# Background work of a hybrid encoder layer in half-width tiles of their own, first statistics by products with ones, folds in another order

## The chip, the cores and the metric

One core of one Trainium2 chip (trn2) runs the kernel. The metric is the device time of one execution in microseconds; all operands are float32 in memory. The kernel before took 2555.42 us (median of three runs, 2549.77 to 2566.65).

## The reference

One encoder layer over 2560 tokens of 1024 channels: a prompt of 512 and a sample of 2048, with the same weights. Heads: 16 for queries, 4 for keys and values, of 64 channels; window of 128 tokens to each side.

```python
h = rmsnorm(x, norm_pre)
z = h @ w_in                       # 1024 -> 6656: pool_u, pool_g, q, k, v, attn_g, merge
pooled = multiscale_pool(pool_u)   # means over 2, 4, 8, 16 tokens, minus u
pb = (pooled @ w_pool_group, by group of 256) * pool_scale * silu(pool_g)
ab = windowed_attention(rope(q), rope(k), v, sink) * silu(attn_g)
m = sigmoid(merge_1) * (pb @ w_pool_proj) + sigmoid(merge_2) * (ab @ w_attn_proj)
y = x + rmsnorm(m @ w_out, norm_post)
```

## The kernel before

**Numbers.** A float32 operand is split into a high part (ScalarE casts, L105) and a low part (VectorE subtracts, L106), `hi_lo`. A product is three matmuls, high x high, high x low, low x high (`mm3`, L141 to L143).

**Phase 1** is the input projection, over three blocks of tokens (`BLOCKS`: 768, 896, 896). A block runs 26 pairs of output units of 128 channels. A pair is seven products (M1 to M7 in `ORDER`, a step each, 12 matmuls of half a block's width) on sums and differences of the weights' and the input's quarters, a scheme of Strassen's kind. The weights of a pair come into an R tile (and half_tile A21, or, from the second block on, ready sums in a Q tile), and each step's weight is split into a w tile. A pair's result goes from PSUM into two z tiles (`Post.start`; L391 adds) and is finished there: rotation of keys and queries (`Rope`), values transposed and stored (`Values.tr_steps`), SiLU, gates, pooling (`Pool`). The first two pairs of a block (keys, values) run step by step in turn, as do the last two. The pooling maps are folded into the weights before and during the first two pairs (`fold`: eight items of three split tiles and 24 matmuls each; results go out over h tiles).

**Background work** hangs beside a pair's steps (`hook(s, i, j, f)`: block, pair, step). `beside` loads at step j and forms at step j + 3. It is: the next block's statistics (sums of squares of x by rows, L222, then `rstd`, and `prep_r`, which spreads the roots over partitions by transposes, L239); the next block's normalised input in seven combinations, stored to memory (`later_load`, `later_form`) and fetched at the change of block through h tiles (`fetch_operand`); the first block's pooling, put off to the second and third (`Pool.again`, `later`); and the splits of the three phase-2 weights (`split_load`, `split_form`). All of it uses z tiles.

**Phase 2** runs the pool projection, attention, attention projection and output projection over blocks of 512 tokens. The change doesn't touch its code.

**Tiles.** z: six of 4 KB per partition; h: four of 2 KB; u: four of 2 KB; R: three of 6 KB; Q: two of 8 KB; w: seven (`NW, NZ, NH, NR = 7, 6, 4, 3`). A tile is free again when its last reader is done, a store's landing included.

**What sets the order.** TensorE's order is the program's, written out by hand; `run` loads weights up to seven w tiles ahead of the step that uses them. The other engines and both DMA queues are ordered before the run by the framework's scheduler, with its own estimates of when tiles come free; so their order is near the program's and not the same (in the trace VectorE forms sums of the pair weights between pieces of the first block's input). At run time each engine takes its list in order. All loads are issued by SP's queue, all stores (`store`, L99) by POOL's.

**Start.** `first` loads the identity and norm_pre, loads the first block's x by rows into six z tiles (L216), squares them on ScalarE, loads the first fold's weights, then the transposed input (four z tiles; two in a spare R, two more z) and two pairs' weights.

## Time and profile before

| | |
|---|---|
| median of three runs | 2555.42 us |
| profiled execution | 2564.07 us, its span 2562.3 us |
| TensorE busy in the span | 2361.5 us |
| VectorE, ScalarE, POOL busy | 1778.3, 1156.8, 446.3 us |
| mean granted clock of TensorE | 0.963 of full |
| moved by DMA | 611.51 MB, mean 239 GB/s |

PE is TensorE, PEld its weight loads, DVE VectorE, ACT ScalarE, POOL GpSimd, SP SyncE, whose queue issues the loads. Busy times include no waiting. A wait is put down to the semaphore that came last.

### The profile page before, as it was taken

How to read it: one execution, taken by the hardware profiler on the slowest of the kernel's cores; microseconds unless marked ns; L12 is line 12 of the kernel's file. 1: busy time of each engine (PE TensorE's matmuls, PEld its weight loads, DVE VectorE, ACT ScalarE, POOL GpSimd, SP SyncE). 2: the span in 40 equal slices, each digit the busy share in tenths (PEclk: the TensorE clock that was granted, in tenths of full speed). 3: DMA queues.
4: the chain of work that ended last, by engine and by line, in shares of the span. 5: the costliest groups of instructions: out<-in, count | busy, mean ns of one | idle time of the engine just before them, and what ended most of it. 6: DMA issues, size and time to landing. Idle time of an engine off the chain costs nothing.

```text
span 2562.3 us, 34370 instructions
## 1 busy us (share of the span) xinstructions
PE 2361.5 (92%) x11668; PEld 2099.0 (82%) x11668; DVE 1778.3 (69%) x3346; ACT 1156.8 (45%) x2461; POOL 446.3 (17%) x961
## 2 busy tenths in 40 slices
PE   4889999989999989578999899899999999989998
PEld 3889999978888888577889887778788878878887
DVE  6667788765677677557677757788488578668732
ACT  5444343634433335233444336566366366546511
POOL 2322222030112110323222201110110111011011
PEclk7989999999999999889999999999999999999999
DMA  7566877664565547667666668777777887867784
GB/s 280 185 243 205 301 256 256 231 211 177 183 244 182 214 176 254 214 231 259 237 239 242 228 223 280 239 260 272 251 254 245 278 271 252 288 227 256 239 299 168
DMA packets 189953, 611.51 MB, mean 239 GB/s; under 512 B 27089, under 2 KB 34513, under 8 KB 179793
## 3 DMA queue, kind: packets, MB, share of 16 engines
q1 hardware_dynamic: 146464, 428.55, 50.6%
q0 software_dynamic: 43312, 180.76, 18.2%
q8 instruction: 92, 1.51, 0.2%
q14 instruction: 85, 0.69, 0.1%
HBM read 428.49 MB, written 180.72 MB: 238 GB/s over the span
## 4 chain that ended last, share of the span: by engine, by line
PE 42%; DMA 8%; DVE 8%; issue 3%; ACT 2%; POOL 1%; SPq 0%; POOLq 0%; DVEq 0%; ACTq 0%
PE ps_g L141 6%; PE ps_g L143 6%; PE ps_g L142 6%; PE ps_s L141 4%; PE ps_s L142 4%; PE ps_s L143 4%; PE ps_t L1019 3%; PE ps_o L1034 2%; PE ps_o L1033 2%; PE ps_s L991 1%; PE ps_s L992 1%; DVE ps_s L995 1%; DVE Q L106 1%; DMA h<-ab 1%; DMA ab<-z 1%
## 5 line engine op out<-in xcount | busy, mean ns | idle before, releaser
L141 PE MATMUL ps_s<-arena,w 128*128 128x448 f32 (+1 forms) x1512 | 556.5, 368 | 112.5 <-DVE z L391 74.1
L142 PE MATMUL ps_s<-arena,w 128*128 128x448 f32 (+1 forms) x1512 | 550.6, 364 | 0.0
L143 PE MATMUL ps_s<-arena,w 128*128 128x448 f32 (+1 forms) x1512 | 549.8, 364 | 0.0
L141 PE MATMUL ps_g<-arena,w 128*128 128x512 f32 (+2 forms) x1264 | 493.8, 391 | 3.4 <-DVE u L860 2.2
L143 PE MATMUL ps_g<-arena,w 128*128 128x512 f32 (+2 forms) x1264 | 478.8, 379 | 0.0
L142 PE MATMUL ps_g<-arena,w 128*128 128x512 f32 (+2 forms) x1264 | 478.5, 379 | 0.0
L141 PEld LDWEIGHTS ps_s<-arena,w 128*128 128x128 f32 x1512 | 291.6, 193 | 143.0 <-DVE z L391 81.0
L105 ACT CAST w<-Q 128x512 fp32r<-128x512 f32 x312 | 192.8, 620 | 367.0 <-PE ps_s L143 323.6
L143 PEld LDWEIGHTS ps_s<-arena,w 128*128 128x128 f32 x1512 | 292.2, 193 | 17.5
L142 PEld LDWEIGHTS ps_s<-arena,w 128*128 128x128 f32 x1512 | 291.9, 193 | 16.8
L143 PEld LDWEIGHTS ps_g<-arena,w 128*128 128x128 f32 x1264 | 240.2, 190 | 35.6
L141 PEld LDWEIGHTS ps_g<-arena,w 128*128 128x128 f32 x1264 | 241.8, 191 | 23.2 <-DVE u L860 2.4
L142 PEld LDWEIGHTS ps_g<-arena,w 128*128 128x128 f32 x1264 | 241.6, 191 | 19.7
L997 ACT ACTIVATE R<-ps_s,nm 128x384 f32<-128x384 f32 (+1 forms) x320 | 179.5, 562 | 147.3 <-DVE nm L995 139.8
L106 DVE TENSOR_TENSOR w<-Q,w 128x512 fp32r<-128x512 f32 x312 | 213.5, 687 | 31.9 <-ACT w L105 20.4
L105 ACT CAST w<-R 128x512 fp32r<-128x512 f32 x234 | 144.8, 620 | 164.3 <-PE ps_s L143 139.9
L106 DVE TENSOR_TENSOR w<-R,w 128x512 fp32r<-128x512 f32 x234 | 160.3, 687 | 80.0 <-ACT w L105 76.8
L995 DVE CUSTOM_DVE_ANT_0 ps_s<-ps_s,mask,nsink 128x384 f32<-128x384 f32 (+1 forms) x320 | 189.0, 593 | 22.4 <-PE ps_s L992 19.7
L106 DVE TENSOR_TENSOR Q<-ps_t,Q 128x512 fp32r<-128x512 f32 x224 | 153.5, 686 | 14.1 <-ACT Q L105 11.7
L1019 PE MATMUL ps_t<-ident,R 128*128 128x128 f32 x896 | 139.9, 278 | 22.9 <-DVE Q L106 19.5
L391 DVE TENSOR_TENSOR z<-ps_s,u 128x448 f32<-128x448 f32 (+1 forms) x144 | 86.2, 598 | 100.8 <-PE ps_s L143 95.3
L1019 PEld LDWEIGHTS ps_t<-ident,R 128*128 128x128 f32 x896 | 111.8, 142 | 49.9 <-DVE Q L106 22.1
(204 smaller groups left out, 3707.9 us busy)
## 6 DMA issues: line engine op xcount, KB each, us to landing
Q<-sw SPq DMA_DIRECT2D x52, 1024.0 KB, 5.5
R<-in_w_h SPq DMA_DIRECT2D x54, 768.0 KB, 6.3
w<-w_pp SPq DMA_DIRECT2D x80, 512.0 KB, 4.9
w<-w_ap SPq DMA_DIRECT2D x80, 512.0 KB, 4.5
w<-w_out SPq DMA_DIRECT2D x72, 512.0 KB, 4.5
sw<-Q POOLq DMA_DIRECT2D x26, 1024.0 KB, 7.2
z<-in_x SPq DMA_DIRECT2D x40, 512.0 KB, 6.0
arena<-q SPq DMA_DIRECT2D x20, 1024.0 KB, 7.4
```

Of the source, the lines that this page charges most:

```text
L105: A.copy(hi, src)
L106: V.tensor_sub(lo, src, hi.bitcast(F32))
L141: T.matmul(o, lhsT=xs[0], rhs=ys[0], start=start, stop=False, skip_group_check=more)
L142: T.matmul(o, lhsT=xs[0], rhs=ys[1], start=False, stop=False, skip_group_check=more)
L143: T.matmul(o, lhsT=xs[1], rhs=ys[0], start=False, stop=stop, skip_group_check=more)
L391: V.tensor_add(dst, acc[:, c], t[:, c])
L991: T.matmul(s, lhsT=q, rhs=st["kh"][:, kc], start=True, stop=False)
L995: V.tensor_tensor_reduce(s, s, mask[:, kb0 * 128:kb1 * 128], -1.0, nsink[:, H:H + 1], ALU.add, ALU.min, nm[:, h:h + 1])
L997: A.activation(P[:, 0:nk], s, AF.Exp, bias=nm[:, h:h + 1], scale=-1.0, accum_out=l[:, h:h + 1])
L1019: T.transpose(tp[:, h * 128:(h + 1) * 128], pr[h][:, i * 128:(i + 1) * 128], cst["ident"])
L1033: T.matmul(o, lhsT=v, rhs=pts[i][:, 0, :], start=i == 0, stop=False)
L1034: T.matmul(o, lhsT=v, rhs=pts[i][:, 1, :], start=False, stop=i == kb1 - kb0 - 1)
```

## The change

- **Tiles.** Statistics (of 512 channels a tile, two sums per row, added by POOL in `rstd`), the later input (half of each half-block a piece), the first block's pooling (two pieces of 400 and 376 columns, `LATE`), and the splits (48 of 512 columns in place of 24 of 1024) go to h tiles. Values go to h, one token tile each. The rotation's high parts reuse t2 and x1; `Silu` uses one tile for both sigmoids. The numbers of tiles are as before.
- **Places.** Statistics beside pairs 4 to 7 (two token tiles each), roots at 7 and 8, the input's eight pieces beside pairs 9 to 12 and 14 to 17; pooling of the first block beside pairs 13 and 18 to 22 of the second block and 4 and 5 of the third, the second half three steps after the first; splits beside pairs 6 to 23 of the third block, three in each of pairs 6 to 17 and two in the rest.
- **First block's statistics.** `first_stats` squares the transposed input (k = 0 to 7) into Q, rope and rbc tiles and sums over partitions by 48 matmuls with a column of ones; the x loads for it are gone. `first_operands` loads all eight transposed tiles at once.
- **Folds.** The first fold's weights follow these loads, the second's come before the pairs' weights; from the fourth item on, raw tiles are h in place of u, and folds within the first two pairs run after steps 1 to 5 in place of 0 to 4.

```diff
...
@@ -116,6 +116,8 @@
+    ones = const.tile([128, 1], F32, tag="ones", name="ones")
+    V.memset(ones, 1.0)
@@ -172,8 +174,8 @@
...
-        def raw_split(src):
-            raw = utile()
+        def raw_split(src, n):
+            raw = utile() if n < 3 else htile()
@@ -182,7 +184,7 @@
...
-                it = Item(lambda g=g, hs=hs: [raw_split(x) for x in (a["w_pool_group"][g], a["wu_t"][2 * g, :, hs], a["wu_t"][2 * g + 1, :, hs])], 3)
+                it = Item(lambda g=g, half=half, hs=hs: [raw_split(x, 2 * g + half) for x in (a["w_pool_group"][g], a["wu_t"][2 * g, :, hs], a["wu_t"][2 * g + 1, :, hs])], 3)
@@ -207,25 +209,46 @@
...
+    def first_stats(k, x):
...
+        t0, t1 = BLOCKS[0][0] // 128, BLOCKS[0][1] // 128
+        n = t1 - t0
+        if k == 0:
+            ssqs["p"] = psum("g")
+        if k % 2 == 0:
+            ssqs["q"] = qtile() if k < 4 else rope_tile().rearrange("p a b -> p (a b)") if k < 6 else row_tile()
+        o = k % 2 * 128 * n if k < 6 else 0
+        sq = ssqs["q"][:, o:o + 128 * n]
+        A.activation(sq, x[:, 0:128 * n], AF.Square)
+        for t in range(n):
+            T.matmul(ssqs["p"][:, t:t + 1], lhsT=sq[:, t * 128:(t + 1) * 128], rhs=ones, start=k == 0 and t == 0, stop=k == 7, skip_group_check=True)
+        if k == 7:
+            ssqs[0] = sb.tile([128, 16], F32, tag="ssq", bufs=2, name="ssq")
+            V.tensor_copy(ssqs[0][:, 0:n], ssqs["p"][:, 0:n])
...
-            ssqs[s] = sb.tile([128, 8], F32, tag="ssq", bufs=2, name="ssq")
+            ssqs[s] = sb.tile([128, 16], F32, tag="ssq", bufs=2, name="ssq")
...
-            res.append(ztile())
-            nc.sync.dma_start(res[-1], a["x"][t * 128:(t + 1) * 128, :])
+            for j in range(2):
+                res.append((t, j, htile()))
+                nc.sync.dma_start(res[-1][2], a["x"][t * 128:(t + 1) * 128, j * 512:(j + 1) * 512])
...
-    def stats_sum(s, ts, xs):
+    def stats_sum(s, xs):
...
-        for t, x in zip(ts, xs):
-            A.activation(x, x, AF.Square, accum_out=ssqs[s][:, t - t0:t - t0 + 1])
+        for t, j, x in xs:
+            i = 8 * j + t - t0
+            A.activation(x, x, AF.Square, accum_out=ssqs[s][:, i:i + 1])
...
+        if s > 0:
+            G.tensor_add(ssq[:, 0:n], ssq[:, 0:n], ssq[:, 8:8 + n])
@@ -266,9 +289,11 @@
...
-        yield
...
+        yield
+        for k in range(8):
+            first_stats(k, h[k])
@@ -303,26 +328,34 @@
...
-    def later_load(s, k):
-        return load_xt(s, k, ztile()), load_xt(s, k + 4, ztile())
...
-    def later_form(s, k, xs):
+    def later_load(s, k, c):
...
+        a_, b = BLOCKS[s]
+        w = (b - a_) // 2
+        res = []
+        for j in range(2):
+            t = htile()[:, 0:w].rearrange("p (i t) -> p i t", i=2)
+            nc.sync.dma_start(t, a["xt"][k + 4 * j, :, a_:b].rearrange("p (i t) -> p i t", i=2)[:, :, c * w // 2:(c + 1) * w // 2])
+            res.append(t)
+        return res
...
+    def later_form(s, k, c, xs):
...
-        l, r = slice(0, w), slice(w, W)
-        ta, tb = ztile(), ztile()
-        normed(s, k, x1)
-        normed(s, k + 4, x2)
-        V.tensor_sub(ta[:, l], x1[:, r], x1[:, l])
-        V.tensor_sub(ta[:, r], x2[:, r], ta[:, l])
-        V.tensor_sub(tb[:, l], x1[:, r], x2[:, r])
-        V.tensor_sub(tb[:, r], x2[:, l], ta[:, r])
-        row = xrow[4 * s + k]
-        store(row[:, 0:w], x1[:, l])
+        cs = slice(c * w // 2, (c + 1) * w // 2)
+        ta, tb = (htile()[:, 0:w].rearrange("p (i t) -> p i t", i=2) for _ in range(2))
+        for x, i in ((x1, k), (x2, k + 4)):
+            V.scalar_tensor_tensor(x, x, cst["gpre"][:, i:i + 1], rbc[s][:, 0:W].rearrange("p (i t) -> p i t", i=2)[:, :, cs], ALU.mult, ALU.mult)
+        V.tensor_sub(ta[:, 0, :], x1[:, 1, :], x1[:, 0, :])
+        V.tensor_sub(ta[:, 1, :], x2[:, 1, :], ta[:, 0, :])
+        V.tensor_sub(tb[:, 0, :], x1[:, 1, :], x2[:, 1, :])
+        V.tensor_sub(tb[:, 1, :], x2[:, 0, :], ta[:, 1, :])
+        row = xrow[4 * s + k].rearrange("p (j t) -> p j t", j=8)
+        store(row[:, 0, cs], x1[:, 0, :])
...
-            store(row[:, (i + 1) * W:(i + 2) * W], t[:, 0:W])
+            store(row[:, 2 * i + 2:2 * i + 4, cs], t)
@@ -472,8 +505,8 @@
...
+            g = ztile()[:, 0:self.W]
...
-                g = ztile()[:, 0:self.W]
@@ -505,9 +538,8 @@
...
-            for c, y in enumerate((t1, x2)):
-                hi = ztile(F32R)[:, 0:W]
-                lo = y.bitcast(F32R)
+            for c, (y, spare) in enumerate(((t1, t2), (x2, x1))):
+                hi, lo = spare.bitcast(F32R), y.bitcast(F32R)
@@ -525,11 +557,11 @@
...
-                    vt = ztile(F32R).rearrange("p (i h d) -> p i h d", i=2, h=4)
...
-                        hi_lo(vt[:, i, :, 0:64], vt[:, i, :, 64:128], src[:, i, :, :])
-                        store(vd[:, :, self.a // 128 + c + i, :], vt[:, i, :, :])
+                        vt = htile().bitcast(F32R).rearrange("p (h d) -> p h d", h=4)
+                        hi_lo(vt[:, :, 0:64], vt[:, :, 64:128], src[:, i, :, :])
+                        store(vd[:, :, self.a // 128 + c + i, :], vt)
@@ -597,39 +620,58 @@
...
+    def pool_mean(k, u, m, tmp, more, edges):
...
+    LATE = (
+        (0, 400, 0, 392, [(8, 0)], [(8, 0, 392, 0)]),
+        (400, 776, 392, 760, [(112, 1), (128, 0)], [(0, 0, 120, 392), (128, 120, 248, 512)]),
+    )
...
+    def late_load(f, j):
+        m0, m1, g0, g1 = LATE[j][:4]
+        u, g = htile(), htile()
+        nc.sync.dma_start(u[:, 0:m1 - m0 + 16], rawu[f][:, m0:m1 + 16])
+        nc.sync.dma_start(g[:, 0:g1 - g0], rawg[f][:, g0:g1])
+        return u, g
...
+    def late_pool(f, j, ug):
+        u, g = ug
+        m0, m1, g0, g1, edges, parts = LATE[j]
+        tmp = [htile()]
+        z, sg = g[:, 0:g1 - g0], tmp[0][:, 0:g1 - g0]
+        A.activation(sg, z, AF.Sigmoid)
+        V.scalar_tensor_tensor(z, z, cst["pscale"][:, f:f + 1], sg, ALU.mult, ALU.mult)
+        x = pool_mean(f // 2, u, m1 - m0, tmp, htile, edges)
+        for xo, go, c, t in parts:
+            V.tensor_mul(x[:, xo:xo + c], x[:, xo:xo + c], g[:, go:go + c])
+            store(pbd[f][:, t:t + c], x[:, xo:xo + c])
...
-        fold0 = fs[0][0]
+        fold0 = fs[0][0], fs[4][0]
@@ -637,12 +679,12 @@
...
-            stats_sum(0, range(n0), stats_load(0, range(n0)))
+            next(forming)
+            fold0[0].load()
+            next(forming)
...
-            fold0.load()
-            next(forming)
+            fold0[1].load()
...
-            next(forming)
@@ -707,27 +749,24 @@
...
-            for i, t in zip((3, 5, 7, 9), range(t0, t1, 2)):
+            for i, t in zip((4, 5, 6, 7), range(t0, t1, 2)):
...
-                beside(s, i, lambda s=s, ts=ts: stats_load(s + 1, ts), lambda x, s=s, ts=ts: stats_sum(s + 1, ts, x))
-            hook(s, 9, 5, lambda s=s: rstd(s + 1))
-            hook(s, 10, 2, lambda s=s: prep_r(s + 1))
-            for k, i in enumerate((11, 13, 17, 19)):
-                beside(s, i, lambda s=s, k=k: later_load(s + 1, k), lambda x, s=s, k=k: later_form(s + 1, k, x))
+                beside(s, i, lambda s=s, ts=ts: stats_load(s + 1, ts), lambda x, s=s: stats_sum(s + 1, x))
+            hook(s, 7, 5, lambda s=s: rstd(s + 1))
+            hook(s, 8, 2, lambda s=s: prep_r(s + 1))
+            for i, (k, c) in zip((9, 10, 11, 12, 14, 15, 16, 17), [(k, c) for k in range(4) for c in range(2)]):
+                beside(s, i, lambda s=s, k=k, c=c: later_load(s + 1, k, c), lambda x, s=s, k=k, c=c: later_form(s + 1, k, c, x))
...
-        first_pools = [x for x in posts[:NPAIR] if isinstance(x, Pool)]
-        for x, (s, i) in zip(first_pools, ((1, 14), (1, 15), (1, 20), (1, 22), (2, 5), (2, 7), (2, 11), (2, 13))):
-            beside(s, i, x.again, lambda _, x=x: x.later())
-        places = [i for i in range(2, NPAIR - 2) if i not in (5, 7, 11, 13)]
-        places = sorted((places + places)[:24])
-        for u in range(24):
-            i = places[u]
-            beside(2, i, lambda u=u: split_load(u), lambda x: split_form(*x), 2 if u and places[u - 1] == i else 0)
+        for f, (s, i) in enumerate(((1, 13), (1, 18), (1, 19), (1, 20), (1, 21), (1, 22), (2, 4), (2, 5))):
+            for j in range(2):
+                beside(s, i, lambda f=f, j=j: late_load(f, j), lambda x, f=f, j=j: late_pool(f, j, x), 3 * j)
+        for u in range(48):
+            beside(2, 6 + u % 18, lambda u=u: split_load(u), lambda x: split_form(*x), u // 18)
@@ -754,28 +793,25 @@
...
-                    prog += fs[:4]
-                    fs = fs[4:]
+                    if j > 0:
+                        prog += fs[:4]
+                        fs = fs[4:]
...
-        z = ztile()
-        if i < 16:
-            n, u = ("w_pp", "w_ap")[i // 8], i % 8
-            nc.sync.dma_start(z, a[n][u])
-            return z, [swp[n, u, h] for h in range(2)]
-        h, u = (i - 16) // 4, (i - 16) % 4 * 2
-        for j in range(2):
-            nc.sync.dma_start(z[:, j * 512:(j + 1) * 512], a["w_out"][h, u + j])
-        return z, [swp["w_out", h, u + j] for j in range(2)]
...
-    def split_form(z, dsts):
-        hi, lo = ztile(F32R), z.bitcast(F32R)
-        hi_lo(hi, lo, z)
-        for j, d in enumerate(dsts):
-            for e, t in enumerate((hi, lo)):
-                store(d[:, e, :], t[:, j * 512:(j + 1) * 512])
+        key = list(swp)[i]
+        h = htile()
+        n, u, j = key
+        nc.sync.dma_start(h, a[n][u, j] if n == "w_out" else a[n][u, :, j * 512:(j + 1) * 512])
+        return h, swp[key]
...
+    def split_form(h, dst):
+        t = htile()
+        hi, lo = t.bitcast(F32R), h.bitcast(F32R)
+        hi_lo(hi, lo, h)
+        for e, x in enumerate((hi, lo)):
+            store(dst[:, e, :], x)
...

```

`pool_mean` is the former body of `Pool.pool` up to the subtraction of u, with tiles and edges as arguments; `Pool.pool` calls it from the second block on.

## Rows read from the trace of the kernel before

**Rows 1.** The page, part 1: busy time, share, instructions of each engine.

```profile
PE 2361.5 (92%) x11668; PEld 2099.0 (82%) x11668; DVE 1778.3 (69%) x3346; ACT 1156.8 (45%) x2461; POOL 446.3 (17%) x961
```

**Rows 2.** Windows: length; PE, PEld, DVE, ACT, POOL busy; clock; DMA share; GB/s.

```profile
0.00:120.00 120.00, 76.15 (x406) 71.97 (x406) 76.95 (x131) 60.53 (x112) 30.08 (x48) 0.83 0.63 227
120.00:165.00 45.00, 33.82 (x158) 32.54 (x159) 34.16 (x57) 18.52 (x33) 19.30 (x37) 0.85 0.72 246
165.00:540.00 375.00, 369.58 (x2063) 363.82 (x2062) 292.63 (x497) 168.53 (x307) 72.71 (x138) 1.00 0.71 251
540.00:582.00 42.00, 28.40 (x122) 24.58 (x121) 21.45 (x33) 12.60 (x25) 13.21 (x25) 0.84 0.58 193
...
750.00:940.00 190.00, 173.02 (x814) 156.40 (x813) 141.62 (x207) 67.99 (x110) 37.61 (x87) 0.96 0.58 205
940.00:1040.00 100.00, 98.87 (x489) 90.70 (x488) 75.20 (x118) 49.85 (x90) 12.23 (x25) 1.00 0.69 237
1040.00:1110.00 70.00, 33.25 (x143) 29.04 (x142) 29.24 (x42) 17.75 (x28) 22.77 (x41) 0.73 0.57 205
1110.00:1510.00 400.00, 374.35 (x1774) 340.54 (x1775) 289.64 (x424) 164.35 (x262) 96.40 (x203) 0.97 0.65 228
```

**Rows 3.** The waits of TensorE: for whom, total, times, longest.

```profile
PE ps_s L141 <- DVE z L391: 74.1, 17, 17.2
```

**Rows 4.** Windows at the start, same columns as rows 2.

```profile
4.00:20.00 16.00, 6.06 (x28) 5.59 (x28) 1.90 (x3) 9.36 (x17) 3.26 (x4) 1.00 1.03 410
...
20.00:70.00 50.00, 27.78 (x141) 25.94 (x141) 44.90 (x80) 28.58 (x58) 11.24 (x16) 0.69 0.66 236
```

**Rows 5.** Timeline, start of the run: start, us, instruction, [idle before, releaser].

```profile
1.65 2.89 SPq L216 DMA_DIRECT2D z<-in_x  x6
...
19.43 0.33 SPq L177 DMA_DIRECT2D u<-in_w_pool_group  x1
...
20.30 0.43 PE L239 MATMUL ps_t<-ident,rcol 128*128 128x128 f32 x2 [0.24 <-ACT h L197]
...
21.18 1.95 DVE L244 SCALAR_TENSOR_TENSOR z<-z,gpre,rbc 128x768 f32<-128x768 f32 x2 [5.89 <-ACT rbc L240]
...
32.62 0.58 PE L141 MATMUL ps_t<-w 128*128 128x256 f32 x1 [11.89 <-ACT w L105]
...
58.06 0.58 PE L141 MATMUL ps_t<-w 128*128 128x256 f32 x1 [7.49 <-ACT w L105]
```

**Rows 6.** Timeline, second and third blocks, ScalarE and TensorE, columns as before.

```profile
577.17 1.06 ACT L222 ACTIVATE z<-z 128x1024 f32<-128x1024 f32 x1 [3.36 <-DMA z<-in_x]
...
1052.78 1.04 ACT L105 CAST z<-z 128x1024 fp32r<-128x1024 f32 x1 [9.23 <-DMA v<-z]
...
1058.23 0.74 PE L141 MATMUL ps_s<-arena,w 128*128 128x448 f32 x1 [17.22 <-DVE z L391]
...
1098.21 0.74 PE L141 MATMUL ps_s<-arena,w 128*128 128x448 f32 x1 [16.46 <-DVE z L391]
```

**Rows 7.** Groups of instructions by form: count, busy us, mean ns, idle before.

```profile
L222 ACT ACTIVATE z<-z 128x1024 f32<-128x1024 f32 x20 | 21.1, 1057 | 13.9 <-DMA z<-in_x 12.0 <-DMA q<-z 1.4
...
L106 DVE TENSOR_TENSOR z<-z 128x1024 fp32r<-128x1024 f32 x24 | 29.4, 1223 | 37.7 <-ACT z L105 37.6
...
L106 DVE TENSOR_TENSOR w<-Q,w 128x512 fp32r<-128x512 f32 x312 | 213.5, 687 | 31.9 <-ACT w L105 20.4 <-PE ps_g L143 1.7
...
L99 POOL DMA_DIRECT2D v<-z x20 | 14.7, 733 | 63.5 <-issue 33.3 <-DVE z L106 19.9 <-DVE Q L368 4.1
```

**Rows 8.** DMA issues: engine, count, KB each, median us from issue to landing.

```profile
R<-in_w_h SPq DMA_DIRECT2D x54, 768.0 KB, 6.3
...
h<-t SPq DMA_DIRECT2D x56, 224.0 KB, 4.2
...
w_out<-z POOLq DMA_DIRECT2D x32, 256.0 KB, 3.9
...
z<-in_xt SPq DMA_DIRECT2D x16, 448.0 KB, 7.9
```

More of the change, by code (lines that the diff above doesn't have):

```diff
@@ L578, in finish @@
             store(rawg[f], g[:, 8:8 + W])
-        def again(self):
-            self.z = [ztile(), ztile()]
-            nc.sync.dma_start(self.z[0][:, 0:self.n], rawu[self.f])
-            nc.sync.dma_start(self.z[1][:, 8:8 + self.W], rawg[self.f])
-        def later(self):
-            self.silu()
-            self.pool()
         def silu(self):
@@ L599, in pool @@
             u, g = self.z
-            k = f // 2
-            w = POOLW[k]
-            edge = cst["edge"]
             m = n - 16
-            x, c0, st = u, 8 - w // 2, 1
-            while st < w:
-                c = m + w - 2 * st
-                if len(self.t) < 2 and st > 1:
-                    self.t.append(ztile())
-                d = self.t[0] if x is not self.t[0] else self.t[1]
-                V.tensor_add(d[:, 0:c], x[:, c0:c0 + c], x[:, c0 + st:c0 + st + c])
-                x, c0, st = d, 0, 2 * st
@@ L612, in pool @@
-            edges = []
-            if s == 0:
-                edges += [(8, 0), (SP, 1), (SP + 16, 0)]
-            if self.last:
-                edges += [(m - 8, 1)]
-            for o, e in edges:
-                G.tensor_mul(x[:, o:o + 8], x[:, o:o + 8], edge[:, k, e, :])
-                G.tensor_scalar(x[:, o:o + 8], x[:, o:o + 8], float(w), None, op0=ALU.mult)
-            V.scalar_tensor_tensor(x[:, 0:m], x[:, 0:m], 1.0 / w, u[:, 8:8 + m], ALU.mult, ALU.subtract)
-            if s == 0:
-                parts = [(8, 8, SP, 0), (SP + 16, SP + 8, W - SP - 8, SP)]
-            else:
-                parts = [(0, 0, m, self.a - 8)]
@@ L625, in pool @@
-            for xo, go, c, t in parts:
-                V.tensor_mul(x[:, xo:xo + c], x[:, xo:xo + c], g[:, go:go + c])
-                store(pbd[f][:, t:t + c], x[:, xo:xo + c])
+            x = pool_mean(f // 2, u, m, self.t, ztile, [(m - 8, 1)] if self.last else [])
+            V.tensor_mul(x[:, 0:m], x[:, 0:m], g[:, 0:m])
+            store(pbd[f][:, self.a - 8:self.a - 8 + m], x[:, 0:m])
+    def pool_mean(k, u, m, tmp, more, edges):
+        w = POOLW[k]
+        x, c0, st = u, 8 - w // 2, 1
+        while st < w:
+            c = m + w - 2 * st
+            if len(tmp) < 2 and st > 1:
+                tmp.append(more())
+            d = tmp[0] if x is not tmp[0] else tmp[1]
+            V.tensor_add(d[:, 0:c], x[:, c0:c0 + c], x[:, c0 + st:c0 + st + c])
+            x, c0, st = d, 0, 2 * st
+        for o, e in edges:
+            G.tensor_mul(x[:, o:o + 8], x[:, o:o + 8], cst["edge"][:, k, e, :])
+            G.tensor_scalar(x[:, o:o + 8], x[:, o:o + 8], float(w), None, op0=ALU.mult)
+        V.scalar_tensor_tensor(x[:, 0:m], x[:, 0:m], 1.0 / w, u[:, 8:8 + m], ALU.mult, ALU.subtract)
+        return x
```

## The prediction

> **What bounds the kernel now.** I read the busy times first: TensorE is busy 92% of the span and no other engine over 69% [rows 1], so only time in which TensorE stands, or runs slower after standing, is to be won. Next the stretches [rows 2], to see where that is. The reader is to compare a stretch's length with its matmuls at the pace of an undisturbed neighbour: 98.87/489 = 0.202 us from 940 to 1040 us, for matmuls of 448 columns (second and third block), and 369.58/2063 = 0.179 us from 165 to 540 us, for 384 columns. The excess is then 45 - 158 x 0.179 = 16.7 us at 120 to 165, 42 - 122 x 0.202 = 17.3 at 540 to 582, 190 - 814 x 0.202 = 25.4 at 750 to 940, 70 - 143 x 0.202 = 41.1 at 1040 to 1110 (where the granted clock averages 0.73 of full), and 400 - 1774 x 0.202 = 41.3 at 1110 to 1510. In the first 120 us TensorE is busy for 76. Third come the waits of TensorE: its longest, 74.1 us in 17 waits, is for VectorE's L391, which takes results out of PSUM into a z tile [rows 3]. Fourth, at the start and at the worst places, the order of time [rows 4 to 6].
>
> **The start.** Transfers move 410 GB/s at a full DMA share from 4 to 20 us [rows 4]. Six loads of x for the first statistics are 3.15 MB, 7.7 us at that rate. Behind them and the transposed input come the second fold's weights: issued at 19.43, and TensorE, idle for 11.89 us for their cast, resumes at 32.62. It idles 7.49 us more for a fold at 58.06 [rows 5]. The change:
> - takes away the loads of x and six squares of 1.06 us [rows 7], and adds eight squares of 128x768: 0.8 us each by width, 1.06 at most, so 6.4 to 8.5 us against 6.4, on an engine that waits for the transfers anyway;
> - adds 48 products with a column of ones. No row shows one. The nearest are the transposes with weights of the same shape, 0.43/2 = 0.21 us [rows 5]; I take 0.2, with ends of 0.1 and 0.4. That is 10 us of TensorE in a stretch where it is busy for 6 of 16 us [rows 4], nearly all of it the first fold. Only the last tile's six, 1.2 us, trail the last tile of the input. The eight transposed tiles (3.15 MB) take the place of the six of x among the transfers, so the root is ready 1 to 2 us later than now; the first fold's matmuls stand between it and the transposes that spread it, and cover that. At 0.4 us the 48 would take 19 us and push the normalisation, now at 21.18 [rows 5], by up to 6 us;
> - moves the second fold's loads ahead of the pair weights: three SP issues and three casts pass the four SP issues of two pairs' weights. Those land some 768 KB / 410 GB/s = 1.9 us later, and no pair starts before the second fold is through. I take 10 of the 11.89 us as won;
> - moves the later folds back by one step and their raw tiles from u, which the first block's T1 pieces hold, to h, which its T2 pieces and the folds' own outputs hold. Of the 7.49 us I count 3.
>
> VectorE is busy 44.9 of the 50 us from 20 to 70 [rows 4], so the operands of the first pairs can't be formed much sooner; that caps this part. Gain **13 us**, between -6 and 25.
>
> **120 to 165 and 540 to 582 us.** The next block's statistics move one pair later and out of z. At 577.17 ScalarE had stood 3.36 us for a load of x into z [rows 6], with a cast of the values behind it in its queue, and VectorE behind that. That wait goes: **11** of 17.3 us (5 to 15). At 120 to 165 the key rotation's z tiles are the larger part, and it needs as many at its end as before: **4** of 16.7 us (0 to 10). What is late next in both is that rotation.
>
> **1040 to 1110 us.** ScalarE stands 9.23 us for "v<-z" before a cast into z, and TensorE then stands 17.22 us; 40 us on it stands 16.46 us once more [rows 6]. Three users of z meet there, and all are moved: the splits of the phase-2 weights start at pair 6 instead of 2 and go to h, the values go to h, the rotation's high part reuses tiles that it has. POOL's v stores stay slow (33.3 us of idle "issue" before 20 of them [rows 7]), but now hold h slots that nothing else wants in those pairs. I take **33** of 41.1 us (20 to 40).
>
> **750 to 940 and 1110 to 1510 us.** Here VectorE's bursts make L391 late: rotations, which are unchanged, and late pools and splits, of which a 1024-wide piece of 1.22 us becomes two of 0.69 [rows 7], with room for L391 between. **8** of 25.4 us (0 to 17) and **10** of 41.3 (0 to 22). The extra work, 24 x (2 x 0.687 - 1.223) = 3.6 us for the splits on VectorE and, by the same overhead of 0.15 us a cut, some 16 us for about 110 more instructions of input pieces and pools, hides in VectorE's idle 31%; uncovered it would cost 20 us. About 56 more DMA issues on SP at 0.33 to 0.48 us [rows 5] and 40 on POOL at 0.73 [rows 7] are 27 and 29 us on queues that are mostly idle (POOL 17% busy), and cost nothing unless a slot wait stands at their head.
>
> **What is added: waits for four h slots.** Until now h had few users between the folds and a change of block. Now an input piece needs four (two loaded, two formed), half of a late pool three or four, a split two; and in pairs 6 to 17 of the third block each pair has three splits, formed one step (12 x 0.202 = 2.4 us) apart. A split's slots come free after a cast and a difference of 0.7 us each, an issue, and a landing 3.9 us after it [rows 7, 8], with the second issue some 6 us in all. The second split's cast then waits 4 us, with weight casts and PSUM copies behind it on ScalarE; the weight casts run up to seven tiles (17 us) ahead, the copies don't. If a quarter of it reaches TensorE that is 12 us, and at 0.3 us for each of 32 input pieces and pool halves 10 more: **-22 us**, between 0 and -50 (all 4 us, 12 times). Behind an SP load that waits for a slot lie the weights of the pair after next.
>
> The transfers themselves shrink in proportion: 224 KB land in 4.2 us where 448 KB take 7.9 [rows 8], so a smaller piece frees its slot sooner; rows of 896 bytes are in no row. The Trainium skill, Perfetto Trace Analysis, section "DMA Optimizations", speaks against such pieces (transfers under 2 KB have a significant overhead each, batching is better). By that rule the waits above would stand at their far end, and the sum at 29 us; by the rows it stands as below.
>
> **Sum.** 13 + 11 + 4 + 33 + 8 + 10 - 22 = 57 us. The profiled execution took 2564.07 us (span 2562.3), 8.65 over the median of 2555.42. 2564.07 - 57 = 2507, and 2498 against the median.
>
> **Rivals.**
> - **The stalls keep their places**, so that the change doesn't do what it says: POOL's slow stores hold h slots as they held z, and only 5 of the 41.1 us go. For it: those 33.3 us of POOL. Against: seven value tiles have four slots to themselves there. 28 us less gain: 2526. Chance 0.15.
> - **The h slots eat the gain**: the waits stand at their far end and the bursts stay, 79 - 18 - 50 = 11 us: 2544. For it: the slots are not increased while most background work moves to them. The skill's rule on small transfers would do this in another way. Chance 0.17.
> - **SP stands behind h, slower than before**: a background load waits for a slot at the head of SP, and the weights behind it miss their cast. Place: 12 pairs with three splits, 8 late pools, 16 input pieces, 36 in all. It decides once SP stands longer than a pair (7 x 2.4 = 17 us) less the weights' landing of 6.3 us [rows 8], some 11 us; past that I put 3 us at each place: 36 x 3 - 79 = 29 us slower, 2584. For it: one meeting of this kind in z costs 17 us now. Against: the longest hold worked out above is 6 us for a split, and some 10 for an input piece with its four stores. Chance 0.10.
> - The forecast has 0.58.
>
> **How the numbers follow.** 1% is about what a measurement of this kernel can tell from no change: under 2530 is faster, over 2581 slower. Faster: the forecast but for 0.02, and 0.10 of the first rival, 0.66. Slower: the third, and 0.02 of the second, 0.12. Between them 0.22. The unknown sizes take the forecast from 2455 (the start, 540 and 1040 us at their best, 80 us, the rest as taken, 22, and no new waits) to some 2530 (all the new waits and the start at nothing); to leave out no more than 2 in 10 the range reaches over the first two rivals to 2553.
>
> **What would show it.** In the changed profile TensorE gets to the second fold by 24 us; no idle of over 6 us stands between 1030 and 1110 us; ScalarE's waits for "v<-z" and "z<-in_x" are gone; TensorE's waits for L391 fall from 74.1 to under 40 us; the new waits, on h, stay under 5 us each. I am wrong if the time from the second block's first matmul to phase 2 does not shrink, if ScalarE stands more than 5 us a pair for stores out of h in pairs 6 to 17 of the third block, or if a product with ones takes over 0.4 us.

## The result, and the profile after

The changed kernel takes 2574.45 us (median of 20 runs, 2566.75 to 2583.45) against 2556.32 us for the kernel before (20 runs): ratio 1.0071, 95% interval 1.0056 to 1.0086, slower by 18 us where 57 us less were forecast. A trace is one execution, which took 2567.62 us for the changed kernel (7 below its median), 2564.07 for the kernel before (8 above), 9 and 13 us above the median in e5 and e8, 7 and 6 below in e6 and e13, and within 8 us in the others, so where to look is read from the traces, and what an edit is worth from the runs.

The page, part 1, of the changed kernel answers to [rows 1]:

```profile
PE 2375.0 (93%) x11764; PEld 2113.1 (82%) x11764; DVE 1783.8 (70%) x3464; ACT 1158.0 (45%) x2517; POOL 482.5 (19%) x1003
```

The windows answer to [rows 2], with the same columns:

```profile
0.00:120.00 120.00, 87.25 (x438) 80.12 (x439) 66.64 (x118) 53.50 (x99) 25.78 (x39) 0.88 0.54 182
...
165.00:540.00 375.00, 346.45 (x1915) 340.82 (x1914) 273.72 (x499) 160.42 (x306) 81.90 (x146) 0.97 0.68 237
...
1040.00:1110.00 70.00, 66.42 (x328) 61.13 (x327) 51.60 (x77) 27.74 (x47) 21.99 (x41) 0.98 0.63 213
1110.00:1510.00 400.00, 353.95 (x1660) 321.45 (x1659) 270.92 (x425) 159.09 (x273) 102.08 (x204) 0.95 0.66 229
```

At 1040 to 1110 us, 328 matmuls are done in place of 143, at a granted clock of 0.98 in place of 0.73: the meeting that held them is gone, as forecast. But on TensorE 165 to 540, which had 5 us of idle time, now has 29, and 1110 to 1510 has 46 in place of 26.

The waits of TensorE (for whom, total, times, longest) answer to [rows 3]. Its longest wait, for results into z (L391 there, L424 here), has all but gone, and waits for sums into u, which VectorE runs in the same queue, stand in its place. These sums are L411 and L419 in the kernel before (first two rows), L444 and L452 in the changed one (the rows below):

```profile
PE ps_s L141 <- DVE u L411: 28.4, 14, 4.7
...
PE ps_s L141 <- DVE u L419: 9.8, 5, 3.3
...
PE ps_s L143 <- DVE u L452: 55.0, 20, 6.4
PE ps_s L143 <- DVE u L444: 37.0, 18, 6.1
...
PE ps_s L143 <- DVE z L424: 7.1, 7, 2.2
```

For the comparison of all runs, the table has stage lengths in us, between the first matmuls of the stages in each trace: the first pair of the first block, its fourth pair, the second block, the third, phase 2, the end.

| run | to pair 1 | to pair 4 | rest of block 1 | block 2 | block 3 | phase 2 |
|---|---|---|---|---|---|---|
| before | 45.9 | 88.6 | 359.8 | 495.4 | 528.2 | 1044.5 |
| after | 48.6 | 95.2 | 380.5 | 486.9 | 515.6 | 1039.1 |
| e1 old start | 45.8 | 81.4 | 382.0 | 491.6 | 527.0 | 1041.3 |
| e2 squares added up | 35.3 | 93.7 | 384.5 | 484.8 | 526.9 | 1042.2 |
| e3 input whole in z | 48.8 | 95.3 | 351.4 | 493.4 | 521.5 | 1043.4 |
| e4 before, new start | 50.6 | 95.1 | 355.8 | 495.1 | 528.9 | 1036.4 |
| e5 e2 and e3 | 35.3 | 93.6 | 354.8 | 492.1 | 525.8 | 1043.3 |
| e6 e5, splits whole in z | 36.3 | 93.9 | 351.8 | 488.5 | 494.3 | 1037.1 |
| e7 e5, splits two steps apart | 37.0 | 94.2 | 352.0 | 491.7 | 522.5 | 1045.6 |
| e8 before, values and rotation | 46.2 | 85.4 | 351.3 | 483.1 | 521.0 | 1044.7 |
| e9 after, input pieces in z | 49.1 | 94.7 | 364.0 | 489.7 | 522.2 | 1047.1 |
| e10 e8, splits from pair 6 | 46.0 | 83.3 | 351.4 | 481.9 | 514.5 | 1037.9 |
| e11 e10, squares added up | 35.8 | 92.1 | 348.0 | 483.0 | 512.2 | 1043.2 |
| e12 e8, late pools in h | 46.0 | 82.6 | 351.6 | 481.0 | 518.2 | 1041.5 |
| e13 e5, split halves in z | 36.0 | 93.6 | 351.8 | 492.6 | 511.4 | 1036.0 |
| e14 e12, splits spread from pair 6 | 46.2 | 83.3 | 352.3 | 483.5 | 498.0 | 1041.1 |

**The start** of the changed kernel, in order of time, answers to [rows 5] (start, duration, instruction, [idle before and its releaser]):

```profile
6.21 10.40 PE L224 MATMUL ps_g<-ones,Q 128*128 128x1 f32 x48 [6.21 <-ACT Q L222]
...
24.38 0.84 ACT L222 ACTIVATE rbc<-z 128x768 f32<-128x768 f32 x1 [11.06 <-PE ps_g L224]
...
25.27 2.63 PEld L224 LDWEIGHTS ps_g<-ones,rbc 128*128 128x128 f32 x12 [1.07 <-ACT rbc L222]
...
36.59 1.94 DVE L267 SCALAR_TENSOR_TENSOR z<-z,gpre,rbc 128x768 f32<-128x768 f32 x2
```

The first row holds 24 products as 48 records: 10.40/24 = 0.43 us a product, twice the price taken. All 48 fill TensorE from 6.21 to 28 us. The last two tiles of squares share the one rbc tile, so the eighth square waits 11.06 us for the seventh's products; TensorE, busy with these and earlier products, loses only 1 us of it. The first fold and the transposes of the roots come behind the products, and the normalisation starts at 36.59 in place of 21.18.

**In the first block**, with the same columns, a load of an input piece (SP), the VectorE instruction that stands for it, and TensorE:

```profile
302.22 0.37 SPq L338 DMA_DIRECT2D h<-in_xt  x1
```

```profile
312.96 0.69 DVE L350 SCALAR_TENSOR_TENSOR h<-h,gpre,rbc 128x448 f32<-128x448 f32 x1 [6.70 <-DMA h<-in_xt]
```

```profile
315.38 0.69 PE L143 MATMUL ps_s<-arena,w 128*128 128x384 f32 x1 [6.42 <-DVE u L452]
```

The load is issued 4.0 us before VectorE is free for it (at 312.96 - 6.70 = 306.26 us), and it lands 10.6 us after its issue, where the median of these loads is 3.6. VectorE stands 6.70 us, the sum behind it comes late, and TensorE idles 6.42. Before the load of the same pair at 299.95 us SP's queue had stood from 292.65 to 297.79 us for a store out of h: the slots make the loads late. But a late issue is half of it. Of the 16 loads in this block four took over 8 us to land, and VectorE's waits for these four are 21.7 of its 29.0 us. Half of the 16 are issued less than 4.2 us before VectorE is free for them, so that a slow landing is not covered.

**In the third block** ScalarE stands for a load into h before a split's cast; behind it in its queue are a rotation's cast and the weight's, and on VectorE a sum out of PSUM. Here the load is issued at 1194.80 us, 2 us after ScalarE was free for it:

```profile
1197.60 0.62 ACT L105 CAST h<-h 128x512 fp32r<-128x512 f32 x1 [4.82 <-DMA h<-in_w_pp]
1198.12 0.93 ACT L105 CAST z<-z 128x896 fp32r<-128x896 f32 x1
```

```profile
1199.09 1.09 DVE L106 TENSOR_TENSOR z<-z 128x896 fp32r<-128x896 f32 x1 [1.70 <-ACT z L105]
...
1201.88 0.62 DVE L444 TENSOR_TENSOR u<-ps_s,s 128x448 f32<-128x448 f32 x1
```

```profile
1202.56 0.74 PE L143 MATMUL ps_s<-arena,w 128*128 128x448 f32 x1 [6.07 <-DVE u L444]
```

VectorE's rotation alone made such sums late before, by 4.7 us at most; with ScalarE's wait on top it reaches TensorE as 6.07 us.

### The profile page after: what moved, and what is told of

It reads as the page before. It is cut to its first block, busy times and chain, and to the rows that moved or that the text cites. A ratio compares the mean times of both kernels' runs of the same rounds, so it can differ in the third digit from the quotient of the medians.

```text
span 2565.9 us, 34997 instructions
## 1 busy us (share of the span) xinstructions
PE 2375.0 (93%) x11764; PEld 2113.1 (82%) x11764; DVE 1783.8 (70%) x3464; ACT 1158.0 (45%) x2517; POOL 482.5 (19%) x1003
## 3 DMA queue, kind: packets, MB, share of 16 engines
q1 hardware_dynamic: 158624, 425.44, 50.6%
## 5 line engine op out<-in xcount | busy, mean ns | idle before, releaser
L105 ACT CAST Q<-ps_t 128x512 fp32r<-128x512 f32 x224 | 130.0, 582 | 36.6 <-PE ps_t L1055 35.1
```

The lines of the kernel that those rows point to most:

```text
L105: A.copy(hi, src)
```

## The experiments

Each was timed against the kernel before on the same chip; medians of different groups are compared by these ratios (the kernel before had 2557.08, 2555.24, 2558.49 and 2554.2 us in e1 to e4, e5 to e8, e9 to e12, e13 and e14). The letters of theories and rivals are those of the expectations, which say what each holds.

### The start

**e4: the kernel before with the change's start alone** (first_stats, load and fold order, raw tiles in h).

```diff
-            stats_sum(0, range(n0), stats_load(0, range(n0)))
+            next(forming)        # all eight transposed tiles
+            fold0[0].load()
+            next(forming)        # first_stats
...
-                    prog += fs[:4]
...
+                    if j > 0:
+                        prog += fs[:4]
```

> The kernel before with the change's start alone (products with ones, fold order, raw tiles in h). Theory A: the fourth pair starts at 142 to 146 us and the whole is 8 to 12 us over before, about 2566. Rival (the start is even): within 4 us of 2556.

2566.44 us, ratio 1.0048 (1.003 to 1.0066); fourth pair at 145.7 us against 134.4. The start costs 9 us where 13 were to be won. Theory A.

**e1: the changed kernel with the old start.** The reverse edit.

> The changed kernel with the start of before: statistics of the first block from x by rows in z tiles, first fold's loads alone ahead of the pair weights, folds after steps 0 to 4, raw tiles all in u. Theory A (the 48 products cost 0.43 us each, which moved the normalisation from 21.2 to 36.6 us and the fourth pair from 134 to 144 us): the fourth pair starts 8 to 12 us earlier than in the changed kernel and the whole falls by about 10 us, to 2564. Rival (the start is even, since the second fold comes earlier; all of the loss lies in waits for h slots later): the fourth pair within 4 us of 144, the whole within 4 us of 2574.

2570.2 us, ratio 1.0058 (1.0033 to 1.0083). The fourth pair starts at 127.1, 17 us earlier, but the third block grew by 11 in the trace, and the whole fell by only some 3 us, which the intervals don't tell from nothing. The 11 need not be the edit's: the changed kernel's 515.6 is the lowest of all traces with split halves in h, and the others have 521.5 to 527.0. Most of the loss lies behind the start.

**e2: the changed kernel with squares added up by VectorE and six products.**

```diff
...
+        if k > 0:
+            V.tensor_add(acc, acc, sq)
...
-        for t in range(n):
-            T.matmul(ssqs["p"][:, t:t + 1], lhsT=sq[:, t * 128:(t + 1) * 128], rhs=ones, ...)
+        if k == 7:     # six products of acc, at the end
...
+            T.matmul(p[:, t:t + 1], lhsT=acc[:, t * 128:(t + 1) * 128], rhs=ones, ...)
```

> The changed kernel with eight squares added up by VectorE and six products with ones in place of 48. Theory A: products take 6 x 0.43 = 2.6 us, the normalisation starts at about 22 to 24 us in place of 36.6, and the whole falls by 12 to 20 us (the second fold stays early): 2555 to 2562. Rival (what delays the first pairs is raw fold tiles and outputs sharing h with the T2 pieces, not the products): the normalisation is earlier, but the fourth pair still starts after 140 us and the whole falls by under 5.

2565.0 us, ratio 1.0035 (1.0019 to 1.0051), 9 us under the changed kernel. Six products took 2.72 us, so 0.45 each, and the first pair starts at 35.3 us, 13 earlier. Theory A for the price, but short of the 12 to 20 us that it put on the whole: in the trace the third block grew by 11 here too. See e11.

### The input pieces

**e3: the changed kernel with the later input whole in z, as before.** `later_load`, `later_form` and their places (pairs 11, 13, 17, 19) are those of before.

> The changed kernel with the later blocks' input formed as before: whole width, in z tiles, beside pairs 11, 13, 17 and 19. Theory B (an input piece needs all four h slots, its loads are issued only when stores out of h have landed, and VectorE stands for them, 41.2 us in 15 waits, 13 us of it while TensorE has nothing to do): the stretch from the fourth pair to the second block falls from 380 to about 362 us, and the whole by 18 to 25, to about 2552. Rival C (small instructions and more stores on POOL are what is slow, or z is short again once the input is back): the stretch stays within 6 us of 380, or the second block grows by what the first wins.

2549.85 us, ratio 0.9978 (0.9963 to 0.9994): 25 us come back, and the rest of the first block goes from 380.5 to 351.4. Rival C isn't excluded yet, since size and place of the tiles changed together.

**e9: the changed kernel with the half-width pieces in z.**

```diff
+        both = ztile()
         for j in range(2):
-            t = htile()[:, 0:w].rearrange("p (i t) -> p i t", i=2)
+            t = both[:, j * 512:j * 512 + w].rearrange("p (i t) -> p i t", i=2)
...
```

> The changed kernel with its half-width input pieces unchanged in number, size and place, but in z: the two loaded halves share one z tile and the two formed ones another. Theory B (the four h slots make the loads late): VectorE's waits for loads of the transposed input fall from 41.2 to under 12 us, the stretch from the fourth pair to the second block from 380 to 352 to 362, the whole by 18 to 27, to about 2551, as with whole pieces. Rival C (small pieces, their instructions and their four stores are slow wherever they lie): the whole within 6 us of 2574.

2560.4 us, ratio 1.0008 (0.9989 to 1.0027): 14 to 16 of the 25 us, between the theories. VectorE's waits for these loads in the stretch to the second block (here for the changed kernel, 144 to 524 us, then e9, 100 to 540):

```profile
DVE h L350 <- DMA h<-in_xt: 29.0, 7, 7.2
```

```profile
DVE z L352 <- DMA z<-in_xt: 4.0, 5, 1.0
```

The slots' part is shown: the waits go from 29.0 to 4.0 us. Slow landings alone don't make them: in e9 the loads of this stretch took longer to land (6.7 us in the median against 4.1), but were issued 9.6 us before VectorE was free for them, in the median, against 4.2. The other 10 us come with the smaller pieces in other places (64 stores on POOL in place of 32, eight places in place of four); which of these isn't settled.

### The splits

**e5: both repairs, e2 and e3 together.**

> Both repairs at once on the changed kernel: squares added by VectorE with six products (15 us earlier at the fourth pair by itself), and the later input whole in z (25 us off the whole by itself). Theories A and B together: the fourth pair at about 129 us, the stretch from there to the second block about 353 us, the whole 2550 - 10 = 2540 us, faster than both kernels. Rival (the gains are of one place: an earlier start is given back where the third block meets its splits, as the run with added squares lost 11 us there): 2547 to 2552.

2537.74 us, ratio 0.993 (0.9906 to 0.9953): the two add up. Faster than both kernels by its interval.

**e6: e5 with the splits whole in z**, beside pairs 6 to 23.

```diff
-        for u in range(48):
-            beside(2, 6 + u % 18, ..., u // 18)
+        for u in range(24):
+            beside(2, 6 + u % 18, ..., 2 * (u // 18))
```

with `split_load` and `split_form` of before.

> The run with both repairs, and the splits of the phase-2 weights in z tiles at full width as before (24, with 1024 columns), beside pairs 6 to 23 of the third block, 18 at step 0 and 6 at step 2. Theory D (ScalarE stands 92 us in the third block before casts into h, for loads into h and stores out of h, and that is where the gain forecast for the third block went; z has room there now): ScalarE's waits before split casts fall under 25 us and the third block falls from about 521 us to 495 to 505, the whole by 15 to 25 against the run with both repairs. Rival E (it is the bursts of VectorE, which 1.22 us pieces make worse, or z is as short as h): the third block stays within 6 us or grows.

2510.36 us, ratio 0.9834 (0.9808 to 0.9859): 27 us less, block 3 from 525.8 to 494.3.

**e13: e5 with the 48 halves in z**, the loaded half and its high part in one z tile.

```diff
-        h = htile()
+        both = ztile()
+        h = both[:, 0:512], both[:, 512:1024]
...
```

> The run with both repairs, its 48 split halves unchanged in number, size and place, but in z: the loaded half and its high part share one z tile. Theory D (h slots make ScalarE stand before split casts): ScalarE's waits for loads and stores before those casts fall from some 90 us to under 30, the third block from 526 to 494 to 505, the whole from 2538 to about 2512, as with whole splits. Rival (size: twice as many instructions, three splits in a pair): the third block over 515 and the whole over 2530.

2528.96 us, ratio 0.9895 (0.9869 to 0.9921): some 9 of the 27 us are the slots, with intervals that overlap (e5 has 0.9906 to 0.9953). ScalarE's waits before split casts at 970 to 1510 us in e5, e13 and e6:

```profile
ACT h L105 <- DMA h<-in_w_pp: 33.9, 7, 6.2
ACT h L105 <- DMA w_pp<-h: 17.6, 11, 4.7
ACT h L105 <- DMA w_out<-h: 13.5, 5, 4.1
ACT h L105 <- DMA h<-in_w_ap: 11.4, 1, 11.4
```

```profile
ACT z L105 <- DMA z<-in_w_out: 47.0, 11, 8.5
ACT z L105 <- DMA z<-in_w_pp: 17.4, 10, 2.9
ACT z L105 <- DMA z<-in_w_ap: 4.3, 3, 3.6
```

```profile
ACT z L105 <- DMA w_out<-z: 6.8, 1, 6.8
ACT z L105 <- DMA z<-in_w_out: 3.7, 3, 1.7
```

In h it waits for stores of splits out of h (31.1 us) and for loads that a slot held back; in z the stores drop out, but loads of three halves a pair, formed three steps after they stand in the program, still come late (68.7 us). As 24 whole pieces (e6) instead of 48 halves, the waits are 12.9 us (85.1 in e5, with smaller rows added to those shown). Theory D's waits of under 30 us for e13 were a miss, and it holds for a third of the price; the rest goes with halves against whole pieces, of which e6 also puts fewer into a pair.

**e7: e5 with the halves of a pair two steps apart.**

```diff
-            hook(s, i, j + 3, lambda: form(box["x"]))
+            hook(s, i + (j + 3) // 7, (j + 3) % 7, lambda: form(box["x"]))
...
-            beside(2, 6 + u % 18, ..., u // 18)
+            beside(2, 6 + u % 18, ..., 2 * (u // 18))
```

> The run with both repairs, with the splits still in h halves, but those of one pair loaded at steps 0, 2 and 4 in place of 0, 1 and 2 (formed three steps on, the last in the next pair). Theory D: a split's two slots come back after some 6 us, and forms 4.9 us apart in place of 2.4 wait about 2.4 us less each; ScalarE's waits before split casts fall from 92 us to 40 to 60 and the third block by 5 to 12 us. Rival E (the waits are not on TensorE's path): waits fall, the third block stays within 4 us.

2545.09 us, ratio 0.9956 (0.9941 to 0.9972), over e5 by 0.0026, where the intervals meet. ScalarE's waits before split casts are 79.7 us, where theory D had 40 to 60, and the third block fell by 3 us in the trace: a miss. The spacing doesn't pay.

### What paid

**e8: the kernel before with values in h and the rotation in its own tiles, and nothing else.**

```diff
-            for c, y in enumerate((t1, x2)):
-                hi = ztile(F32R)[:, 0:W]
+            for c, (y, spare) in enumerate(((t1, t2), (x2, x1))):
...
+                hi, lo = spare.bitcast(F32R), y.bitcast(F32R)
...
-                    vt = ztile(F32R).rearrange("p (i h d) -> p i h d", i=2, h=4)
...
+                        vt = htile().bitcast(F32R).rearrange("p (h d) -> p h d", h=4)
...
```

> The kernel before with two parts of the change alone: values to h tiles, one token tile each, and the rotation's high parts in t2 and x1. Splits stay in z from pair 2 on. Theory F (the meeting at 1040 to 1110 us was made by z tiles of values and rotation held for POOL's stores): the two stalls of 17 us shrink to under 8 in all and the third block falls from 528 to about 500, the whole by 20 to 28 us, to about 2532. Rival G (the splits beside pairs 2 and 3 make it, and only their move ends it): the stalls stay over 15 us, the whole within 8 us of 2556.

2520.84 us, ratio 0.987 (0.9846 to 0.9895), 34 us less than before. All three blocks win (8.5, 12.3 and 7.2 us in the trace), and one of the two long stalls stays in the third, at 1037 us, so theory F's 8 us for both was a miss there. Its cause is the third user of z: VectorE waits for a store of the splits before L391 (both rows: e8, 960 to 1520 us):

```profile
PE ps_s L141 <- DVE z L391: 33.2, 8, 17.8
```

```profile
DVE z L391 <- DMA w_pp<-z: 12.4, 1, 12.4
```

**e10: e8 with the splits, whole and in z, from pair 6 on.**

```diff
-        places = [i for i in range(2, NPAIR - 2) if i not in (5, 7, 11, 13)]
+        places = [i for i in range(6, NPAIR - 2) if i not in (7, 11, 13)]
```

> The kernel before with values in h, the rotation's high parts in t2 and x1, and the splits, whole and in z, moved to start beside pair 6 in place of 2. In the run without the move one wait of 17.8 us was left in the third block. Theory F: values and rotation are one half of the meeting, the splits the other; the wait goes, the third block falls from 521 to 500 or less, the whole from 2521 to 2498 to 2508. Rival: the splits, moved closer together, meet late pools instead, and the whole stays within 6 us of 2521.

2516.8 us, ratio 0.9836 (0.9812 to 0.986). The stall goes (row below, same window), but the block falls only to 514.5. That splits, now two in each of nine pairs, make other sums late is argued and not shown here; e14 bears on it.

```profile
PE ps_s L141 <- DVE z L391: 18.1, 6, 5.4
```

**e11: e10 with e2's start**, raw fold tiles in u and folds in their old places.

> The run before this one and the start with added squares and six products, the second fold's loads early, but later folds in their old places with raw tiles in u. Theory A: first pair at 35 us and the fourth at 117 to 122 (131 to 132 without), the whole 8 to 14 us lower than the run before this one, about 2492. Rival (VectorE's forming of the first operands bounds the first pairs): the fourth pair within 4 us of 131 and the whole within 4 us.

2516.97 us, ratio 0.9832 (0.9807 to 0.9856): nothing, the rival's numbers. The first pair starts 10 us earlier, the fourth at 127.9 against 129.4. In the trace of e11 the wait has only moved to a later fold. It is VectorE that sets it: it works on operands and sums of weights without a break from 40 to 55 us (27.25 us busy from 30 to 60), and SP's queue stands from 46.82 to 51.41 us, until VectorE is through with the first operand in u, before it loads that fold's raw tile:

```profile
58.72 0.58 PE L143 MATMUL ps_t<-w 128*128 128x256 f32 x1 [13.12 <-ACT w L105]
```

**e12: e8 with the late pools in h halves, as in the change.**

> The kernel before with values in h, rotation in t2 and x1, and the first block's late pools as in the change: 16 halves in h, beside its pairs. Theory D (every use of h that needs three or four slots in a pair stands for its own stores): block 2 grows from 483 us by 3 to 8 and the whole is 2524 to 2532. Rival (the late pools are few and the gain of shorter bursts shows): the whole falls by 4 to 10, to about 2513.

2522.59 us, ratio 0.9857 (0.9833 to 0.9881): no difference from e8 that the intervals show, for or against.

**e14: e12 with its splits, whole and in z as there, spread over pairs 6 to 23** (there from pair 2 on, without pairs 5, 7, 11 and 13).

> The run with values in h, rotation in t2 and x1 and late pools in h (2522.6), with the splits whole in z spread over pairs 6 to 23, one in each and a second in the first six. If it is the spread (one piece a pair leaves VectorE's gaps for L391): the third block falls from 518 to 492 to 500 and the whole to about 2500. Rival (the start or the statistics in h made the run with whole splits the fastest): the third block over 510, the whole within 8 us of 2522.

2508.01 us, ratio 0.9807 (0.9779 to 0.9835). Block 3 falls from 518.2 to 498.0, so it is the places of the splits and neither the start nor the statistics. Both things about the places count, as far as the traces tell: the start at pair 6, which ends the long stall (e10), and the spread, one in each pair and a second in six where e10 has a second in nine. This is the lowest median of all runs, level with e6 by the intervals, and 2.6% below the changed kernel by the two ratios (0.9807/1.0071 = 0.974).

## Why the prediction was wrong

The sum closes, by runs on different bases and so only roughly: the start -9 where +13 was put; values, rotation and moved splits +42 (e10) where 11 + 4 + 33 = 48; the shorter pool bursts 0 (e12) and no gain shown from split bursts where 18; new waits and small pieces -25 (e3) and -27 (e6 against e5) where -22. That is -19 us; -18 was measured. That it closes so well is in part luck: the intervals of these runs are 4 to 6 us to either side.

- **The start: the step that failed first.** "I take 0.2, with ends of 0.1 and 0.4", from transposes with weights of the same shape: a product with ones took 0.43 us in two records. Even the far end was below it. The condition named, "if a product with ones takes over 0.4 us", came true. Two things were not in that row. A transpose leaves one record, a product two. And the transposes of [rows 5] ran at the faster of two paces: at 19.46 us they start 0.108 us apart, when the fold's matmuls of 256 columns had just gone over from a start every 0.21 us to one every 0.12. In the changed kernel such matmuls start 0.21 us apart behind the products and go over to 0.12 only at 32.2 us, so the products ran at the slower pace (weight loads of the products and of the fold behind them took 0.33 us alike, and 0.19 after 32.2 us), although the granted clock reads 1.00 from 6 to 28 and from 28 to 34 us. By the ratio of the paces a product would take some 0.24 us at the faster one, an estimate: no run has it there. The Trainium skill, FP8 and Floating Point Precision, section "TensorE Precision Notes", says that true float32 goes through the array in 4 passes; the trace shows two records a product, and no run here shows four. The shared rbc tile was not in the working at all; it put 11.06 us into ScalarE's queue, but cost TensorE 1 us, as shown above. The gain side failed as well: TensorE came to the second fold at 35.28 us and not by 24. With six products it came there at 23.81 (e2), and e11 shows that 10 us won at the first pair are lost again by the fourth. The prediction named the cap itself, VectorE's 44.9 of 50 us, and counted 13 us all the same.
- **The waits on h and the smaller pieces: right in kind, mis-sized by more than half.** -22 with an end at -50; e3 and e6 give 25 + 27 = 52 together. By e9 and e13 the slots are some 14 and 9 us of that, 23 in all, about what was put; that it was split otherwise (12 for the splits, and 0.3 us for each of 16 input pieces, 5 in all) makes the agreement partly luck. What failed is the rest, some 29 us: that the extra work "hides in VectorE's idle 31%" and that the extra issues "cost nothing unless a slot wait stands at their head", which it did. For the input pieces the working left out how VectorE stands: a piece that needs all four slots can't be loaded while the one before is stored, so its load is issued just before it is wanted, and VectorE stood 29.0 us before the second block. It also left out that a smaller piece brings one more load and one more place where a queue can stand; what of that makes the 29 us isn't settled.
- **The small-transfer rule.** The row said that half the bytes take half the time to land, and in the median that held: input pieces landed in 3.6 us in the changed kernel, 5.4 in e9, against 7.9 for the whole pieces before. But single ones took up to 10.6 us, and that cost where the load was issued late and an engine stood for it with its queue in order. The waits came to the far end that the rule would give; whether any of it is an overhead of small transfers, no run here shows, and the row alone didn't price it.
- **1040 to 1110 us: right.** No idle over 3.21 us stands there, waits for L391 fell from 74.1 to 7.1 us, those for "v<-z" are gone. The time from the second block's first matmul to phase 2 did shrink, from 1023.6 to 1002.5 us in the traces, so the loss stands before it. But the reason was wider than put: values and rotation without any other edit are worth 34 us in all three blocks (e8), and the stretches at 120 and 540 us, of which the second was given to the statistics, won by it too. In e8, 223 matmuls are done from 120 to 165 us in place of 158, and 180 from 530 to 572, in the same part of its block as the 122 of 540 to 582 before.
- **The bursts**: no gain. Splits in halves made block 3 longer; pool halves changed nothing.
- **The rivals.** "The h slots eat the gain" had the sizes of the waits (-50) and of the bursts (none), with 2544 us, though slots are less than half of those 52 us. Against its 11 us of gain, the start's 22 us are what took the time to the other side of the kernel before; that the start would lose was in no rival, and the range left that side out. "SP stands behind h" came nearest in time (2584), and SP's queue does stand for stores out of h, for up to 13.9 us; but the pairs' weights were there for their casts: ScalarE waits 3.5 us in all for loads into Q and R.

What stays open: which part of a small input piece costs the other 10 us, and how much of the 18 us of split halves is their number and how much the three-step lead.

## What to carry to other kernels

Ease a scarce buffer by freeing uses that hold it through a store, before cutting work into pieces for another pool: two small edits gave 34 us, and the rest of the change took back these and 18 more. A pool whose one user needs every slot has no load in flight far ahead, so the engine that forms it stands whenever a transfer lands late (7 waits for 16 loads here); count slots for the piece in work and for the next. Price an operation that the trace lacks by a row of its own number type and at the pace that TensorE has in that stretch, not by the shape of its weights alone, and let the range reach past the nearest row.

## What was not expected of the hardware

A float32 product of a 128x128 weight with one column took 0.43 us at the slower pace of TensorE (two records, 0.21 us apart), as long as 2 matmuls of 448 columns at the pace of 0.202 us from 940 to 1040 us. Forty-eight of them filled TensorE for 21 us of 22 (6 to 28 us), and it stayed at the slower pace all that time and for 4 us of the fold behind them, with a granted clock that reads 1.00: the pace showed only in how far apart the matmuls start.
